# Empty expert slots left out of indirect transfers, and low weight parts split by rows, in a one-core Hyena, Fourier and mixture-of-experts block

## Chip, cores and metric

The kernel runs on one core of one Trainium2 chip. The metric is the device time of one execution in microseconds (us). About 0.3% can be told from no change.

## What is computed

One block for 2048 tokens of 1024 values: a mixer, then a mixture of experts, then a last norm. Cut to what matters here:

```
h    = rmsnorm(x)                        # 2048 x 1024
proj = h @ w_in                          # 3*512 Hyena columns, 512 Fourier columns
y1   = long convolution (FFT of 4096) of gated Hyena columns, 512 columns
y2   = real part of a 2-D FFT over tokens and 64 columns, 8 groups
x    = x + head_rmsnorm([y1, y2]) @ w_out
tok  = rmsnorm(x)
each token: best of 4 groups, best 2 of its 8 experts -> 4096 (token, weight) pairs, 32 experts
out[t] += weight * (silu(tok[t] @ w_gate[e]) * (tok[t] @ w_up[e])) @ w_down[e]
result = rmsnorm(x + out)
```

## The kernel before, in words

Products that must be exact to fp32 are made from a high and a low part (fp32r): hi x hi, hi x lo, lo x hi. The program is written in one order; a scheduler then puts each engine's instructions in a fixed order, earlier written work first where several are ready, and buffers with a tag are handed on when the last reader of the old content is through.

1. **Projection (0 to about 422 us).** `piece` (L323) multiplies cut weights with the transposed tokens `hhi`, `hlo`. The Hyena columns get a short convolution, go through DRAM and through the first step of the FFT (`ufirst`, L561).
2. **Residues and Fourier products (422 to 618 us).** `fourier(h, i)` (L674) makes 128 tokens x 256 columns of half `h` with 24 matmuls (L680): for each of 8 row blocks `d` of the weights hi x hi, then with the low weights, then with the low tokens. Half 0 has 16 products, the first six right at 422 us; half 1 has 16. Between them stand the 32 spectrum residues (`residue`, L756): nine matmuls each (L754; 15 for residue 0), two loads, casts and copies on ScalarE (ACT), six operations on VectorE (DVE, L782 once for each residue but the first) and one on GpSimd (POOL). In the program one residue follows each product, eight ahead of it at the start. The tables `su`, `sk`, `si` (L740) are loaded by POOL; their part 0 is read by residue 0 alone.
3. **Weights of a half.** `fweights(h)` (L664) takes the buffer "whl" for the high parts `wh` (two buffers) and "wl" for the low parts `wl` (one buffer), and for each column group `g` of 128: loads `wr` into "wraw" (one buffer) by SyncE's queue (SP, L670), cuts eight 128x128 pieces with ACT (`wh`, L309) and writes eight low pieces with DVE (`wl`, L310). `fweights(1)` stands in the program after product 4 of half 0.
4. **End of that stage.** With residue 31 done, buffers are opened for the Fourier mixer: `cs1` (a table, in the pool "fq"), `h5` (in "wraw"), `r0` (in the first row of `lg`). `mid`, two sums of `h5`, is made at L1093 and L1094 in the next pool.
5. **Mixer outputs and routing (618 to about 945 us).** `route` picks experts and ranks their tokens; `order` puts the experts in the order of their use, full ones first, the least filled of each group last. Then four lists over [128 slots x 32 experts] are written: `gia`, `gib` (rows to gather; an empty slot reads row 0) and `sia`, `sib` (rows to add to; an empty slot names one of 160 spare rows behind the 2048 rows of `X2`).
6. **Experts (945 to 1594 us, end at 1674 us).** For each expert: gather of 128 rows of 4 KB (`xg`, L987), for 18 of them also 32 overflow rows in quarters (`xo`, L990), transposes, `gate_up` (L1722), `down` (L1815), then a GpSimd DMA that adds the result into `X2` (L1821), and one for the overflow (L1758). Each waits for the one before. Weights stream in by SP. The last two experts (30, 31) run undivided: `ahead` (L1620) gathers their rows of `X2` once all additions have landed, `bulk` (L1581) reads all of `X2` again (L1588), norms and writes it; `finish` (L1626) adds the two experts' part, writes it to `X2` (L1635) and their output rows go out by a scatter (L1874) that has a bounds check already.

## Time and profile before

| | us |
|---|---|
| median of 3 runs | 1671.64 (1668.62 to 1673.2) |
| the profiled execution | 1675.47 |
| its span, first to last instruction | 1673.7 |
| mean granted TensorE clock, share of full | 0.982 |
| projection, to the first Fourier product | 0 to 422 |
| residues and Fourier products | 422 to 618 |
| mixer outputs and routing | 618 to 945 |
| experts and last norm | 945 to 1674 |

The stages' borders are read from the order of instructions in time. A row of a window gives, for a stretch of time, each engine's busy time in us, with the number of instructions that start in it in brackets; then the granted TensorE clock as a share of 2.4 GHz, the mean busy share of the 16 DMA engines, and GB/s. A row of instructions in time gives start, duration, engine, line, operation, output and input, a count, and in brackets the idle time before it and what ended that. Matmuls overlap, so the distance of their starts, not their duration, is what one costs.

### The profile page before, as it was taken

What the parts mean: (1) busy time and instruction counts of PE and PEld (TensorE: products, weight loads), DVE (VectorE), ACT (ScalarE), POOL (GpSimd) and SP (SyncE); (2) the same over time, 40 slices, a digit from 0 to 9 for tenths busy, and PEclk for the clock granted to TensorE, in tenths of its full rate; (3) what the DMA queues carried; (4) which work ended last, traced back from release to release, by engine and by line L of the source; (5) the groups of instructions that cost most, each with busy time, mean ns of one, the idle gap of its engine ahead of it and who ended that gap; (6) DMA issues with size and microseconds to landing.
All of it is one profiled execution on the core that took longest, in us unless ns stands there. A gap on an engine that the chain in (4) does not pass through costs nothing.

```text
span 1673.7 us, 27233 instructions
## 1 busy us (share of the span) xinstructions
PE 1574.7 (94%) x8995; PEld 1200.8 (72%) x8995; DVE 1192.6 (71%) x2162; ACT 1031.0 (62%) x1746; POOL 438.7 (26%) x515
## 2 busy tenths in 40 slices
PE   7999999999998999999999999999999999999992
PEld 5767776778887787876666567777777777777740
DVE  7667756533499966555877877888878888888825
ACT  8445667555698844414444467777777777777732
POOL 0202444332233220103434331222222222221112
PEclk9999999999998999999999999999999999999996
DMA  7245677699765587668778689999999999999997
GB/s 265 66 133 156 191 214 217 189 312 256 212 197 189 176 257 232 203 222 229 230 225 320 227 315 337 337 353 361 343 325 338 351 369 340 333 340 349 378 383 281
DMA packets 202447, 449.77 MB, mean 269 GB/s; under 512 B 27037, under 2 KB 83066, under 8 KB 201280
## 3 DMA queue, kind: packets, MB, share of 16 engines
q1 hardware_dynamic: 129176, 316.25, 53.5%
q0 software_dynamic: 39568, 106.07, 22.4%
q10 hardware_dynamic: 33560, 25.69, 4.7%
q8 instruction: 72, 1.18, 0.3%
q14 instruction: 71, 0.58, 0.1%
HBM read 346.05 MB, written 103.17 MB: 268 GB/s over the span
## 4 chain that ended last, share of the span: by engine, by line
PE 73%; DVE 11%; ACT 5%; DMA 4%; issue 3%; POOL 1%; ACTq 0%; DVEq 0%; POOLq 0%; SPq 0%
PE pa L1722 20%; PE py L1815 10%; PE psm L323 9%; PE psd L1055 8%; PE po L1738 4%; PE pm L680 3%; PE po L1754 2%; PE pstr L1685 2%; PE pa L1719 1%; DMA xt<-in_x 1%; POOL acc L513 1%; PE psEO L1075 1%; PE psm L680 1%; PE pstr L1779 1%; PE pseo L1138 1%
## 5 line engine op out<-in xcount | busy, mean ns | idle before, releaser
L1538 DVE TENSOR_TENSOR l<-w,h 128x1024 fp32r<-128x1024 f32 x352 | 425.7, 1223 | 80.0 <-ACT h L1537 60.4
L1537 ACT CAST h<-w 128x1024 fp32r<-128x1024 f32 x352 | 368.9, 1049 | 106.9 <-PE pa L1722 75.2
L323 PE MATMUL psm<-hhi,wt 128*128 128x512 f32 x768 | 249.9, 396 | 0.7 <-ACT hhi L425 0.5
L1722 PE MATMUL pa<-h,xh 128*128 128x512 f32 x464 | 185.6, 400 | 0.2 <-issue 0.2
L1722 PE MATMUL pa<-l,xh 128*128 128x512 f32 x464 | 181.9, 392 | 0.0
L1722 PE MATMUL pa<-h,xl 128*128 128x512 f32 x464 | 181.6, 391 | 0.0
L323 PEld LDWEIGHTS psm<-hhi,wt 128*128 128x128 f32 x768 | 144.7, 189 | 35.9 <-issue 4.0
L323 PE MATMUL psm<-hlo,wt 128*128 128x512 f32 x384 | 151.7, 395 | 0.4 <-DVE hlo L426 0.2
L987 POOL DMA_INDIRECT xg<-XR,gia x30 | 45.9, 1529 | 295.0 <-PE pstr L1685 154.9
L1722 PEld LDWEIGHTS pa<-h,xh 128*128 128x128 f32 x464 | 87.0, 188 | 30.9 <-issue 12.0
L1722 PEld LDWEIGHTS pa<-h,xl 128*128 128x128 f32 x464 | 87.1, 188 | 20.2 <-DVE xl L1690 0.4
L1722 PEld LDWEIGHTS pa<-l,xh 128*128 128x128 f32 x464 | 87.1, 188 | 18.4 <-issue 0.4
L1815 PE MATMUL py<-l,sh 128*128 128x512 f32 x240 | 98.6, 411 | 0.0
L1815 PE MATMUL py<-h,sh 128*128 128x512 f32 x240 | 97.6, 407 | 0.7 <-ACT sh L1783 0.7
L1815 PE MATMUL py<-h,sl 128*128 128x512 f32 x240 | 96.3, 401 | 0.0
L323 PEld LDWEIGHTS psm<-hlo,wt 128*128 128x128 f32 x384 | 72.8, 189 | 16.6 <-DVE hlo L426 1.0
L1758 POOL DMA_INDIRECT X<-yo,sib x18 | 37.2, 2064 | 166.0 <-DVE l L1538 110.9
L748 POOL TENSOR_TENSOR yl<-yl,yh 128x512 fp32r<-128x512 f32 x32 | 48.6, 1522 | 108.2 <-ACT yh L747 82.8
L1738 PE MATMUL po<-w,xot 128*32 128x256 f32 x1152 | 66.9, 381 | 0.0
L513 POOL TENSOR_TENSOR acc<-ab,acc 128x512 f32<-128x512 f32 x32 | 48.2, 1507 | 69.0 <-ACT ab L512 67.8
L347 ACT COPY u<-psm 128x512 f32<-128x512 f32 x48 | 28.1, 586 | 53.0 <-PE psm L323 52.7
L680 PE MATMUL pm<-wh,hhi 128*128 128x256 f32 x208 | 59.9, 289 | 0.8 <-ACT wh L309 0.8
(495 smaller groups left out, 3655.8 us busy)
## 6 DMA issues: line engine op xcount, KB each, us to landing
w<-in_w_gate SPq DMA_DIRECT2D x128, 512.0 KB
w<-in_w_up SPq DMA_DIRECT2D x128, 512.0 KB
w<-in_w_down SPq DMA_DIRECT2D x120, 512.0 KB
xt<-in_x SPq DMA_DIRECT2D x31, 512.0 KB
de<-in_c_decay SPq DMA_DIRECT2D x32, 256.0 KB
YK<-yk ACTq DMA_DIRECT2D x32, 256.0 KB
z<-zT POOLq DMA_DIRECT2D x32, 256.0 KB, 5.9
YZ<-yz SPq DMA_DIRECT2D x64, 128.0 KB
```

The lines of the kernel that those rows point to most:

```text
L323: T.matmul(pm, wt[:, a, d, :], b[q][:, d, :], start=n == 0, stop=n == 23)
L513: G.tensor_tensor(KS["acc"], ab, KS["acc"], op=ALU.add)
L680: T.matmul(pm, a[q][:, d, P * o:P * o + P], b[:, d, :], start=n == 0, stop=n == 23)
L748: e.tensor_tensor(yl, y, yh, op=ALU.subtract)
L987: G.indirect_dma_start(xg_[e], None, XR, bass.IndirectOffsetOnAxis(ap=ga[:, e:e + 1], axis=0))
L1055: T.matmul(pd, a[:, c, :], b[:, c, 512 * h:512 * h + 512], start=n == 0, stop=n == 11)
L1537: cuts.append(A.copy(h, raws[n]))
L1538: V.tensor_tensor(l, raws[n], h, op=ALU.subtract)
L1722: T.matmul(pa[m], x[:, 4 * k + c, :], y[:, f], start=d == 0 and q == 0, stop=d == 7 and q == 2)
L1738: T.matmul(po_[e][32 * j:32 * j + 32, 256 * m:256 * m + 256], xoT[e][:, b % 2, 2 * k + b // 2, :], w[:, 256 * j:256 * j + 256], start=b == ...
L1758: G.indirect_dma_start(X4, bass.IndirectOffsetOnAxis(ap=sib[:, d:d + 1], axis=0), yo, None, compute_op=ALU.add)
L1815: T.matmul(py[i], x[:, c, :], y[:, f], start=c == 0 and q == 0, stop=c == 3 and q == 2)
```

## The change

Two things are changed, and memory is laid out anew around the second.

- **Empty slots.** `gia` and `gib` are gone; gathers use `sia` and `sib`, whose empty slots point past the last token. All gathers, additions and writes of experts get a bounds check, so that rows out of bounds are left out. The gathers of the first two experts keep their own list (`gfix`) without such rows.
- **Low weights.** `wl` is split by rows: row blocks 0 to 3 in "wl" (now two buffers of half the size), row blocks 4 to 7 in "wm" (one buffer). `fweights` goes by row halves: load of both column groups, eight cuts, and for the first half the eight low pieces; the second half's low pieces are written by `rest`, called where the half's first product begins.
- **Layout.** Part 0 of the three tables goes to "wraw" (for `si` half of it), the rest to smaller tiles; nine loads in place of three. `cs1` goes to "wraw", `h5` and `r0` to "wl", `mid` to the first row of `lg`, made in two halves by `middle`: half 0 with residue 31 done, half 1 after product 14.

```diff
-        gia = cp.tile([P, NE], I32, name="gia")
-        gib = cp.tile([P, NE], I32, name="gib")
...
             def fweights(h):
                 wh = wp.tile([P, 8, 256], F32R, tag="whl", bufs=2, name="wh")
-                wl = wx.tile([P, 8, 256], F32R, tag="wl", bufs=1, name="wl")
-                for g in range(2):
-                    wr = wp.tile([P, 8, P], F32, tag="wraw", bufs=1, name="wr")
-                    S.dma_start(wr, Wp[2 * h + g])
-                    cutg(wh[:, :, P * g:P * g + P], wl[:, :, P * g:P * g + P], wr)
-                fw[h] = wh, wl
+                wls = [wx.tile([P, 4, 256], F32R, tag="wl", bufs=2, name="wl")]
+                def low(j):
+                    for d in range(4):
+                        for g in range(2):
+                            sl = slice(P * g, P * g + P)
+                            V.scalar_tensor_tensor(wls[j][:, d, sl], wr[:, g, d, :], g1[:, 4 * j + d:4 * j + d + 1],
+                                                   wh[:, 4 * j + d, sl], op0=ALU.mult, op1=ALU.subtract)
+                for j in range(2):
+                    wr = wp.tile([P, 2, 4, P], F32, tag="wraw", bufs=1, name="wr")
+                    for g in range(2):
+                        S.dma_start(wr[:, g], Wp[2 * h + g][:, 4 * j:4 * j + 4, :])
+                    for d in range(4):
+                        for g in range(2):
+                            A.activation(wh[:, 4 * j + d, P * g:P * g + P], wr[:, g, d, :], AF.Copy,
+                                         scale=g1[:, 4 * j + d:4 * j + d + 1])
+                    if j == 0:
+                        low(0)
+                def rest():
+                    wls.append(wx.tile([P, 4, 256], F32R, tag="wm", bufs=1, name="wm"))
+                    low(1)
+                    return wh, wls
+                fw[h] = rest
...
-            wh, wl = fw.pop(0)
+            wh, wl = fw.pop(0)()
...
-            for x, n in ((su, "c_su"), (sk, "c_sk"), (si, "c_si")):
-                G.dma_start(x, I[n].rearrange("x p h c -> p x h c"))
+            t0 = wp.tile([P, 1024], F32R, tag="wraw", bufs=1, name="t0")
+            su = [[t0[:, 192 * a:192 * a + 192] for a in range(2)]]
+            sk = [[t0[:, 384 + 256 * a:640 + 256 * a] for a in range(2)]]
+            si = [[t0[:, 896:1024], fp.tile([P, P], F32R, name="si0")]]
+            for x, n, w in ((su, "c_su", 192), (sk, "c_sk", 256), (si, "c_si", P)):
+                y = fp.tile([P, 2, w], F32R, name=n)
+                G.dma_start(y, I[n][1])
+                for a in range(2):
+                    G.dma_start(x[0][a], I[n][0, :, a])
+                x.append([y[:, a] for a in range(2)])
...
+            def middle(h):
+                x, y = (h5[k].rearrange("p (g c) -> p g c", g=2) for k in range(2))
+                g = slice(2 * h, 2 * h + 2)
+                V.tensor_tensor(v4(mid[:, 0:264])[:, g], x[:, :, 0:66], y[:, :, 0:66], op=ALU.add)
+                V.tensor_tensor(v4(mid[:, 264:512])[:, g], x[:, :, 66:128], y[:, :, 66:128], op=ALU.subtract)
...
                 if h:
-                    wh, wl = fw.pop(h)
+                    wh, wl = fw.pop(h)()
...
-                            css = {1: [fq.tile([P, 2, 2, 2, P], F32R, name="cs1")]}
+                            css = {1: [wp.tile([P, 2, 2, 2, P], F32R, tag="wraw", bufs=1, name="cs1")]}
...
-                            x = wp.tile([P, 2, 512], F32, tag="wraw", bufs=1, name="h5")
+                            x = wx.tile([P, 4, 256], F32, tag="wl", bufs=2, name="h5")
...
         def gather(e, part=(0, 1)):
-            ga, gb = (gfix[:, 0], gfix[:, 1]) if e < NFIX else (gia, gib)
+            ga, gb = (gfix[:, 0], gfix[:, 1]) if e < NFIX else (sia, sib)
...
-                G.indirect_dma_start(xg_[e], None, XR, bass.IndirectOffsetOnAxis(ap=ga[:, e:e + 1], axis=0))
+                G.indirect_dma_start(xg_[e], None, XR, at(ga[:, e:e + 1]), bounds_check=L - 1, oob_is_err=False)
...
-                        for u, x in enumerate((gia, gib)):
-                            first_rows(x, lt[:, u], u)
-                        V.tensor_copy(wsl, lt[:, 2:4])
...
+                        V.tensor_copy(wsl, lt[:, 2:4])
...
-                G.indirect_dma_start(za, None, X2, at(sia[:, e:e + 1]))
+                G.indirect_dma_start(za, None, X2, at(sia[:, e:e + 1]), bounds_check=L - 1, oob_is_err=False)
...
-                G.indirect_dma_start(X2, bass.IndirectOffsetOnAxis(ap=sia[:, e:e + 1], axis=0), yt, None, compute_op=ALU.add)
+                G.indirect_dma_start(X2, at(sia[:, e:e + 1]), yt, None, compute_op=ALU.add,
+                                     bounds_check=L - 1, oob_is_err=False)
```

The gather of `xo`, the addition of `yo` and the write of `za` change in the same way, the uses of the tables and of `wl` follow the new tiles, and L1093 and L1094 are gone.

## Rows read from the trace of the kernel before

**Rows 1.** The page's first part: busy us (share of the span) x instructions.

```profile
PE 1574.7 (94%) x8995; PEld 1200.8 (72%) x8995; DVE 1192.6 (71%) x2162; ACT 1031.0 (62%) x1746; POOL 438.7 (26%) x515
```

**Rows 2.** Windows, all engines: stretch, PE, PEld, DVE, ACT, POOL, clock, DMA, GB/s.

```profile
1008.00:1554.00 546.00, 546.00 (x3608) 416.75 (x3608) 450.96 (x476) 405.00 (x482) 125.57 (x78) 1.00 0.97 345
1586.00:1650.00 64.00, 52.58 (x142) 26.16 (x140) 28.87 (x57) 29.83 (x58) 14.44 (x18) 0.92 1.03 389
```

**Rows 3.** Instructions in time, PE: neighbouring matmuls of L754 and of L680.

```profile
443.64 0.39 PE L754 MATMUL U<-yh,su 128*128 128x512 f32 x1
443.87 0.40 PE L754 MATMUL U<-yl,su 128*128 128x512 f32 x1
...
600.06 0.28 PE L680 MATMUL pm<-wl,hhi 128*128 128x256 f32 x1
600.18 0.28 PE L680 MATMUL pm<-wh,hlo 128*128 128x256 f32 x1
```

**Rows 4.** Windows of L680 alone, then of L754 alone: PE, clock, DMA, GB/s.

```profile
500.00:520.00 20.00, 11.18 (x70) 1.00 0.65 208
520.00:545.00 25.00, 10.61 (x58) 0.80 0.60 188
...
590.00:618.00 28.00, 22.50 (x173) 1.00 0.77 239
...
500.00:520.00 20.00, 13.59 (x42) 1.00 0.65 208
520.00:545.00 25.00, 11.39 (x32) 0.80 0.60 188
...
590.00:618.00 28.00, 4.44 (x15) 1.00 0.77 239
```

**Rows 5.** Windows, all engines, before the change of halves and over it.

```profile
500.00:520.00 20.00, 19.46 (x112) 16.49 (x111) 19.41 (x28) 19.07 (x36) 9.08 (x5) 1.00 0.65 208
520.00:545.00 25.00, 19.08 (x90) 15.47 (x88) 20.74 (x39) 17.18 (x36) 7.47 (x5) 0.80 0.60 188
```

**Rows 6.** Low pieces (DVE), load (from the chain that ended last) and cuts (ACT).

```profile
521.40 3.20 DVE L310 SCALAR_TENSOR_TENSOR wl<-wr,vecs,wh 128x128 fp32r<-128x128 f32 x8
...
524.63 6.26 DMA wr<-Wp
...
530.91 2.44 ACT L309 ACTIVATE wh<-wr,vecs 128x128 fp32r<-128x128 f32 x8 [0.95 <-DMA wr<-Wp]
...
531.35 1.22 DVE L310 SCALAR_TENSOR_TENSOR wl<-wr,vecs,wh 128x128 fp32r<-128x128 f32 x4 [1.70 <-ACT wh L309]
...
533.32 1.14 DVE L310 SCALAR_TENSOR_TENSOR wl<-wr,vecs,wh 128x128 fp32r<-128x128 f32 x4
```

**Rows 7.** Instructions in time, DVE: L782, two successive residues, and the fifth after.

```profile
516.39 0.68 DVE L782 TENSOR_TENSOR ks<-U,ks 128x512 f32<-128x512 f32 x1
...
520.75 0.68 DVE L782 TENSOR_TENSOR ks<-U,ks 128x512 f32<-128x512 f32 x1
...
551.79 0.68 DVE L782 TENSOR_TENSOR ks<-U,ks 128x512 f32<-128x512 f32 x1
```

**Rows 8.** Instructions in time: first table load (POOL), first matmul of residue 0.

```profile
423.54 0.71 POOL L740 DMA_DIRECT2D su<-in_c_su  x1 [1.08 <-DVE cv L339]
...
442.24 0.39 PE L754 MATMUL K<-yh,sk 128*128 128x512 f32 x1
```

**Rows 9.** The end: POOL's additions, SP's reads in time; the checked scatter's group.

```profile
1589.14 2.39 POOL L1821 DMA_INDIRECT X<-yt,sia  x1 [6.53 <-ACT h L1537]
1600.77 1.55 POOL L1821 DMA_INDIRECT X<-yt,sia  x1 [9.24 <-DMA X<-yt,sia]
...
1610.07 16.57 SPq L1588 DMA_DIRECT2D xt<-X  x16
...
L1874 POOL DMA_INDIRECT out_y<-oa,sia x2: 981/1002/1023, 1659.3 to 1663.3; - x2
```

More of the change, by code (lines that the diff above doesn't have):

```diff
@@ L678, in fourier @@
                 for d in range(8):
-                    for a, b in ((hhi, wh), (hhi, wl), (hlo, wh)):
-                        T.matmul(pm, a[q][:, d, P * o:P * o + P], b[:, d, :], start=n == 0, stop=n == 23)
+                    for a, b in ((hhi, wh[:, d, :]), (hhi, wl[d // 4][:, d % 4, :]), (hlo, wh[:, d, :])):
+                        T.matmul(pm, a[q][:, d, P * o:P * o + P], b, start=n == 0, stop=n == 23)
                         n += 1
@@ L775, in residue @@
                     kp, up = kp[0], up[0]
-                    prod(kp, lambda a: sk[:, r, a, 64:192], kh, kl)
-                    prod(up, lambda a: su[:, r, a, 64:192], uh, ul)
+                    prod(kp, lambda a: sk[r][a][:, 64:192], kh, kl)
+                    prod(up, lambda a: su[r][a][:, 64:192], uh, ul)
                     lo, hi = slice(0, 64), slice(64, P)
@@ L885, in build @@
                         reverse(i - 13)
+                    if h and i == 14:
+                        middle(1)
                     while j0(i, h):
@@ L903, in build @@
                                 G.dma_start(css[1][0][:, c], I["c_ldft"][1][:, c, :, 0:2])
-                            x = wp.tile([P, 2, 512], F32, tag="wraw", bufs=1, name="h5")
+                            x = wx.tile([P, 4, 256], F32, tag="wl", bufs=2, name="h5")
                             for k in range(2):
-                                h5[k] = x[0:1, k]
-                                S.dma_start(h5[k][:, 0:256], RM[1 - k][3][0:1, 0:256])
+                                h5[k], r0[k] = x[0:1, k], x[0:1, 2 + k]
+                                S.dma_start(h5[k], RM[1 - k][3][0:1, 0:256])
                             lg = gp.tile([P, NT, 36], F32, name="lg")
                             lst = gp.tile([P, 2, 5, NE], F32, name="lst")
-                            x = lg.rearrange("p a b -> p (a b)")
-                            for k in range(2):
-                                r0[k] = x[0:1, 256 * k:256 * k + 256]
+                            mid = lg.rearrange("p a b -> p (a b)")[0:1, 0:512]
+                            middle(0)
                             jm = lst.rearrange("p a b c -> p (a b c)")[:, 0:P]
@@ L1090, in build @@
                 S.dma_start(altr, I["c_altr"])
-                mid = fo.tile([1, 512], F32, name="mid")
-                V.tensor_tensor(v4(mid[:, 0:264]), v4(h5[0])[:, :, 0:66], v4(h5[1])[:, :, 0:66], op=ALU.add)
-                V.tensor_tensor(v4(mid[:, 264:512]), v4(h5[0])[:, :, 66:128], v4(h5[1])[:, :, 66:128], op=ALU.subtract)
                 def pseo():
@@ L1615, in bulk @@
                 return [lambda g=g: end(g) for g in (4, 8, 12)]
-            def at(rows):
-                return bass.IndirectOffsetOnAxis(ap=rows, axis=0)
             def ahead(e):
                 za = fa.tile([P, D], F32, tag="q", bufs=2, name="za")
-                G.indirect_dma_start(za, None, X2, at(sia[:, e:e + 1]))
+                G.indirect_dma_start(za, None, X2, at(sia[:, e:e + 1]), bounds_check=L - 1, oob_is_err=False)
                 return za
@@ L1634, in finish @@
                     A.activation(oa[:, f], za[:, f], AF.Square, accum_out=ss[:, i:i + 1])
-                G.indirect_dma_start(X2, at(sia[:, e:e + 1]), za, None)
+                G.indirect_dma_start(X2, at(sia[:, e:e + 1]), za, None, bounds_check=L - 1, oob_is_err=False)
                 V.tensor_tensor(ss[:, 0:1], ss[:, 0:1], ss[:, 1:2], op=ALU.add)
```

20 lines of the change are left out of this document (10 added, 10 removed).

## The prediction, on record before the changed kernel ran

> **What bounds the kernel now.** I read the page first, then the windows, then the stage in which the diff moves work. The page [rows 1] says TensorE (PE) is busy 94% of the span, so time is gained only where PE stands still or runs at half clock. The windows of the whole core [rows 2] split the second half: from 1008 to 1554 us PE is busy for 546.00 of 546 us, and from 1586 to 1650 us the DMA share is 1.03 with PE at 52.6 of 64 us. So the gathers and additions of the expert loop lie behind PE until the last experts, and then the DMA engines and a chain of waits set the end.
>
> The stage from 442 to 618 us runs two kinds of work: 32 spectrum residues (L756, matmuls of L754, most of DVE and ACT) and the Fourier products (L680), which fill PE. Between neighbouring matmuls of one kind the starts lie 0.12 us apart for L680 and 0.23 us for L754 [rows 3]. Multiply by the counts of the windows [rows 4]: in 500 to 520 us PE did 70 x 0.12 + 42 x 0.23 = 18.1 us of work, 90%. In 520 to 545 us it did 58 x 0.12 + 32 x 0.23 = 14.3 us of 25, so 10.7 us are lost; at the 10% of the stretch before it would have been 2.5 us. **The hole costs PE about 8.2 us.** Part is standing still, part the clock: its mean is 0.80 there [rows 5], that is, for a while the lower level of 1.2 GHz in place of 2.4 GHz, after PE had run out of work.
>
> What made the hole: the low weights of column half 1 may be written only when the last product of half 0 has read the one buffer "wl". At 521.40 DVE writes the first eight pieces (3.20 us), only then is "wraw" free for the second load, which takes 6.26 us by the chain, then ACT cuts eight pieces (from 530.91 us, 2.44 us), then DVE writes the last eight [rows 6]. The residue cadence shows the same: L782 comes every 4.36 us (516.39 to 520.75), but its next five periods take 31.04 us [rows 7].
>
> **The change part by part.** *Weights of half 1.* The sixteen cuts and sixteen lows stay, but are ordered by rows: lows of rows 0 to 3 go to a second buffer "wl", with nothing of half 0 in their way; the load of rows 4 to 7 and its cuts follow. Only the eight lows of rows 4 to 7 ("wm", one buffer) still wait for the last product of half 0. So the load and the cuts leave the hole. What stays is eight DVE pieces, 3.20 us by the row. PE meanwhile has the first half of the next product, 12 matmuls x 0.12 = 1.4 us, and then waits at most 1.8 us; queued behind the lows on DVE are the residues' products, and PE's L754 waits for those. Term: 8.2 - 1.8 = 6.4 us. Bounds: below, 3.7 us, DVE's own account (31.04 - 5 x 4.36 = 9.24 us beyond the cadence, of which 3.20 + 1.22 + 1.14 = 5.56 us are lows that must be done anyway); above, the whole 8.2 us. I take 6.4, because the stage ends on PE: from 590 to 618 us it holds 173 products of L680 and only 15 of L754 [rows 4], so what counts is how much of L680 is left when the residues are through. That the moved work costs nothing elsewhere rests on DVE and ACT finding room between 450 and 520 us; they are busy 19.41 and 19.07 of 20 us there [rows 5], so this cover is thin, and a rival below takes it away.
>
> *SP and POOL.* Four loads of 512 KB become eight of 256 KB, some 0.3 us of SP's queue each, with slack. Those of half 1 now stand behind the release of t0, the tables of residue 0 in "wraw", so after that residue, near 450 us; the hole is at 520, hence nothing. The tables become nine loads on POOL instead of three, six of them behind the lows of half 0 that read "wraw". Before, the first was issued at 423.54 us and read at 442.24 [rows 8]: 18 us of room for six more issues of about 0.7 us each, so nothing again; cover gone, residue 0 slips one for one. cs1 goes to "wraw", its loads free to start before the residues end. The two sums "mid" become four smaller ones, earlier, on DVE after the residues; nothing either way.
>
> *Index lists.* Three DVE operations on 32 columns go, sia comes first; gather 2 reads it while PE is dense. The bounds check is already on the last scatter: 1.00 us on POOL, where an unchecked addition takes 1.55 [rows 9]. No cost.
>
> *Empty slots.* In the dense stretch, nothing. At the end: the additions of experts 28 and 29 are issued at 1589.14 and 1600.77 us, the second when the first has landed, and the reads of the result begin at 1610.07, when the second has [rows 9]: 20.9 us in line, ahead of the whole ending. Routed on the host, the reference fills 116 and 113 of the 128 slots of these two experts (103 and 91 of the last two), so 27 of 256 rows go. If the time between issue and landing, less 2.4 and 1.6 us of POOL, follows rows, that is 16.9 x 27/256 = 1.8 us; if what lands last is another row, nothing. The profile has no addition with fewer rows; I take 0.9, half way, and keep 0 and 1.8.
>
> The Trainium skill, "DMA: Bandwidth & Descriptors", section "The descriptor swizzle", deals the partitions of a 128-partition transfer in groups of four to the engines, so the empty slots from 113 up would all lie with four of sixteen engines, and the others would keep eight rows each. By that rule the last landing stays where it is, the term is 0 and the sum 6.4 us; no run here shows an engine's own rows.
>
> **Sum.** 6.4 + 0.9 = 7.3 us. The profiled execution took 1675.47 us (span 1673.7 and 1.8 around it) and stands 3.8 us above the median of 1671.64; it would come to 1668.2. Against the median: **1664.3 us**. About 0.3%, or 5 us, is what a measurement of this kernel can tell from no change.
>
> **Rivals.** *DVE sets the end of the stage* (chance 0.2). The second half of the lows is now written into the program after the residues of half 0, so DVE, full as it is, may take those residues first; the next product waits half done, PE idles beside the residues, and only DVE's 3.7 us are saved. For it: DVE at 97%. Against: 173 products after the residues. Time: 1671.6 - 3.7 - 0.9 = 1667.0.
>
> *Nothing arrives* (0.2). What PE gains at 545 us is lost behind it: from 590 to 618 us there are waits of other stages to meet, and no row shows how the rest takes an earlier start; or the order of instructions shifts and gives back as much. For it: PE loses 10% in 500 to 520 us as well, without such a cause. Time: 1671.6 less 0 to 2, so 1670.6.
>
> *Slower* (0.11). The place is ACT and DVE between 450 and 520 us. If cuts and lows of half 1 hold up the residues there one after the other, 2 x 2.44 + 3.20 = 8.1 us are added to the residue chain, the last eight lows still cost 3.2 at 520, and if the interleaving then falls out of step by one cadence, 4.4 more: 15.7 us against the 9.2 that the residues lost before, so 6.5 us more, less 0.9: 1677.2. It decides from 9.2 us of added delay on. For it: both engines at 95% and more. Against: the pieces come in ones, and L680 stays free to fill PE.
>
> *Forecast* (0.49): the hole closes but for a wait of up to 1.8 us.
>
> **How the numbers follow.** The forecast alone spans 1660 to 1666. Faster by over 0.3% is most of it, a third of the first rival (its 4.6 us lie at the bound), and little else: 0.58. Within: 0.31. Slower: 0.11. The range takes in the upper bound with both terms whole (8.2 + 1.8, and 3 us for a stage that runs on better than I know: 1658.5) and the rival without gain with a run above the median: 1673.0; the slower rival is what is left out, and some above the low end.
>
> **What would show it.** Right: in the profile after, lows of rows 0 to 3 near 460 us; no load of Wp after 500; eight lows alone at the change of halves, no PE wait over 2 us there, clock 1.00 throughout; 25 us there hold over 75 products of L680; the last L680 some 6 us earlier, and the start of the dense expert stretch as much. At the end, the distance from the addition of expert 28 to the first read of the result falls from 20.9 to about 20 us, or stays. Wrong: lows of rows 4 to 7 spread over later residues (first rival); the last L680 at 617 us with the hole gone (second); L782 periods of over 5 us between 450 and 520 (third); or tables landing after 442 us.

## The result and the profile after

The changed kernel takes 1683.18 us (median of 5 runs, 1680.28 to 1685.39) against 1671.64 us before (5 runs, 1668.62 to 1675.34): a ratio of 1.0062 with a 95% interval of 1.0041 to 1.0083. It is 11.5 us slower by the medians and 10.4 by the ratio, where 7 us faster was forecast. The profiled execution has a span of 1682.6 us, 8.9 more than before.

TensorE (PE) does the same work in the same busy time, by the first part of the page (it answers to [rows 1]):

```profile
PE 1574.5 (94%) x8995; PEld 1200.8 (71%) x8995; DVE 1196.6 (71%) x2161; ACT 1032.4 (61%) x1746; POOL 441.9 (26%) x521
```

So the 8.9 us are time in which PE stands still. To find them I count each stage from the first residue matmul (442.24 us before, 442.0 after; over all runs it moves between 438.7 and 444.6 us although nothing ahead of it differs much). The stage that the change edits ends for the rest of the program when the mixer can use its result; I take the first matmul of the row of alternating signs (`nyquist`, L1106 before, L1139 after), "Nyquist" below, 181.0 us after the first residue matmul before and 190.2 after: 9.2 us. From there to the order of the experts the kernel after is 0.9 us longer, the dense expert stretch 1.5 us shorter, the ending 0.5 us longer, and its start 0.2 us earlier: together the 8.9 us.

Residues and products both end late. The groups of the last residue products and of the Fourier products in the kernel before (L754, L680), then after (L779, L699); the two times are the first and the last start:

```profile
L754 PE MATMUL zp<-ph,si x64: 387/397/628, 448.5 to 599.8; 128*128 128x512 f32 x64
...
L680 PE MATMUL pm<-wh,hlo x208: 274/283/415, 448.1 to 617.3; 128*128 128x256 f32 x104
```

```profile
L779 PE MATMUL zp<-ph,c_si x62: 387/397/730, 454.6 to 609.8; 128*128 128x512 f32 x62
...
L699 PE MATMUL pm<-wh,hlo x208: 274/283/419, 447.1 to 626.4; 128*128 128x256 f32 x104
```

The windows of all engines say where (columns as in [rows 5]; the third row answers to its second):

```profile
465.00:485.00 20.00, 13.38 (x39) 7.31 (x38) 19.18 (x29) 18.93 (x38) 6.34 (x5) 0.91 0.55 167
500.00:520.00 20.00, 18.03 (x102) 14.77 (x101) 17.52 (x26) 18.03 (x38) 4.68 (x4) 1.00 0.62 197
520.00:545.00 25.00, 21.78 (x128) 18.10 (x127) 24.05 (x32) 21.24 (x40) 8.57 (x7) 1.00 0.58 184
546.00:588.00 42.00, 37.24 (x212) 32.22 (x211) 35.89 (x52) 30.96 (x58) 9.74 (x8) 0.92 0.61 187
```

The kernel before, in the first and the last of these stretches:

```profile
465.00:485.00 20.00, 19.28 (x108) 15.82 (x107) 19.07 (x27) 18.52 (x35) 7.10 (x5) 1.00 0.61 191
...
546.00:588.00 42.00, 38.74 (x227) 32.53 (x226) 39.95 (x55) 37.00 (x68) 12.12 (x10) 1.00 0.55 167
```

From 520 to 545 us the old hole is gone: 128 matmuls where there were 90, and the clock at 1.00. In its place stand two others. **The first hole** is at 465 to 485 us: 39 matmuls, where the kernel before has 108. PE's instructions in time show that not one Fourier product runs for 20.3 us, and that the clock falls to its lower level (a residue matmul of 0.40 us takes 0.63):

```profile
465.01 0.28 PE L699 MATMUL pm<-wh,hlo 128*128 128x256 f32 x1
...
480.22 0.63 PE L779 MATMUL zp<-pl,c_si 128*128 128x512 f32 x1
...
485.30 0.33 PE L699 MATMUL pm<-wh,hhi 128*128 128x256 f32 x1
```

PE waits for ScalarE (ACT). Products go into two buffers "pm", and a buffer is free when ACT has copied it out (L713). ACT's instructions in time: cuts of half 1 (L681) and then the first copy since 442 us, 20 us after the two buffers were full:

```profile
454.01 0.69 ACT L681 ACTIVATE wh<-wr,vecs 128x128 fp32r<-128x128 f32 x2
...
474.43 1.28 ACT L681 ACTIVATE wh<-wr,vecs 128x128 fp32r<-128x128 f32 x4
...
479.95 0.40 ACT L681 ACTIVATE wh<-wr,vecs 128x128 fp32r<-128x128 f32 x1
...
484.82 0.37 ACT L713 COPY rt<-pm 128x256 f32<-128x256 f32 x1
```

It is the fixed order of ACT's instructions that does this, not a wait. Of that order, condensed, only the cuts of half 1, the copies of products and the `zs` copy of each residue, before:

```
L309 ACTIVATE wh<-wr  (eight, the last ahead of the third of these)
L694 COPY rt<-psm     (the first six products)
L793 COPY zs<-zp      (residue 0)
L694 COPY rt<-pm      (first product in pm)
L793 COPY zs<-zp      (residues 1, 2, 3)
L694 COPY rt<-pm      (second)
L694 COPY rt<-pm      (third)
```

and after:

```
L713 COPY rt<-psm     (the first six products)
L818 COPY zs<-zp      (residue 0)
L681 ACTIVATE wh<-wr  x2
L818 COPY zs<-zp      (residues 1, 2, 3, 4)
L681 ACTIVATE wh<-wr  x5
L818 COPY zs<-zp      (residue 5)
L681 ACTIVATE wh<-wr
L818 COPY zs<-zp      (residue 6)
L713 COPY rt<-pm      (first product in pm)
L818 COPY zs<-zp      (residue 7)
L713 COPY rt<-pm      (second)
```

**The second hole** is at 546 to 588 us: PE 37.24 of 42 us at a mean clock of 0.92 (before 38.74 at 1.00). It is not a stretch without products, but one in which PE has gaps. There the lows of row blocks 4 to 7 come one by one between the pieces of residues, over 14 us, where before eight came in one block of 3.20 us [rows 6]. DVE's instructions of L672 in time:

```profile
543.51 0.70 DVE L672 SCALAR_TENSOR_TENSOR wm<-wr,vecs,wh 128x128 fp32r<-128x128 f32 x1
...
550.52 0.60 DVE L672 SCALAR_TENSOR_TENSOR wm<-wr,vecs,wh 128x128 fp32r<-128x128 f32 x2
...
554.64 1.28 DVE L672 SCALAR_TENSOR_TENSOR wm<-wr,vecs,wh 128x128 fp32r<-128x128 f32 x1
...
557.54 0.34 DVE L672 SCALAR_TENSOR_TENSOR wm<-wr,vecs,wh 128x128 fp32r<-128x128 f32 x1
```

The ending is as it was. POOL's additions and SP's reads in time, as in [rows 9]: 20.55 us from the addition of expert 28 to the first read, 20.93 before.

```profile
1597.91 2.00 POOL L1850 DMA_INDIRECT X<-yt,sia  x1 [6.92 <-ACT h L1568]
1609.45 1.55 POOL L1850 DMA_INDIRECT X<-yt,sia  x1 [9.54 <-DMA X<-yt,sia]
...
1618.46 16.61 SPq L1619 DMA_DIRECT2D xt<-X  x16
```

### The profile page after: what moved, and what is told of

The parts are those of the page before. It is cut to its first block, busy times and chain, and to the rows that moved or that the text cites. A ratio compares the mean times of both kernels' runs of the same rounds, so it can differ in the third digit from the quotient of the medians.

```text
span 1682.6 us, 27360 instructions
## 1 busy us (share of the span) xinstructions
PE 1574.5 (94%) x8995; PEld 1200.8 (71%) x8995; DVE 1196.6 (71%) x2161; ACT 1032.4 (61%) x1746; POOL 441.9 (26%) x521
## 4 chain that ended last, share of the span: by engine, by line
PE 70%; DVE 11%; DMA 6%; ACT 5%; issue 4%; POOL 2%; SPq 1%; ACTq 0%; POOLq 0%; DVEq 0%
PE pa L1750 19%; PE py L1844 10%; PE psm L321 8%; PE psd L1091 8%; PE po L1766 4%; PE pm L699 2%; PE po L1782 2%; PE pstr L1713 2%; POOL acc L511 2%; PE pa L1747 1%; DMA cs<-in_c_ldft 1%; PE psm L699 1%; PE pstr L1808 1%; PE psEO L1111 1%; PE pseo L1171 1%
## 5 line engine op out<-in xcount | busy, mean ns | idle before, releaser
L1023 POOL DMA_INDIRECT xg<-XR,sia x30 | 48.3, 1611 | 293.4 <-PE pstr L1713 168.4
L1750 PEld LDWEIGHTS pa<-h,xl 128*128 128x128 f32 x464 | 87.2, 188 | 20.2 <-issue 0.4
L321 PEld LDWEIGHTS psm<-hlo,wt 128*128 128x128 f32 x384 | 72.5, 189 | 16.6 <-DVE hlo L424 1.0
L773 POOL TENSOR_TENSOR yl<-yl,yh 128x512 fp32r<-128x512 f32 x32 | 45.0, 1409 | 119.5 <-ACT yh L772 109.1
L699 PE MATMUL pm<-wh,hhi 128*128 128x256 f32 x208 | 59.4, 286 | 0.0
```

The lines of the kernel that those rows point to most:

```text
L321: T.matmul(pm, wt[:, a, d, :], b[q][:, d, :], start=n == 0, stop=n == 23)
L699: T.matmul(pm, a[q][:, d, P * o:P * o + P], b, start=n == 0, stop=n == 23)
L773: e.tensor_tensor(yl, y, yh, op=ALU.subtract)
L1023: G.indirect_dma_start(xg_[e], None, XR, at(ga[:, e:e + 1]), bounds_check=L - 1, oob_is_err=False)
L1750: T.matmul(pa[m], x[:, 4 * k + c, :], y[:, f], start=d == 0 and q == 0, stop=d == 7 and q == 2)
```

## The experiments

The table gives each kernel's ratio to the kernel before, measured on the same chip, with its 95% interval; that ratio times 1671.64 us, to be held against the times in the expectations (the kernel before has medians of 1674.7 to 1676.3 us beside these runs); and three times from its trace in us after its own first residue matmul: the start of the last residue matmul, of the last Fourier product, and Nyquist. The three times are those of one profiled execution each and hold to 0.1 us as readings. *halfrows*, the last experiment, ran once and is not in the table.

| kernel | ratio (interval) | us | residue | product | Nyquist |
|---|---|---|---|---|---|
| before | 1 | 1671.6 | 157.6 | 175.1 | 181.0 |
| after | 1.0062 (1.0041 to 1.0083) | 1682.0 | 167.8 | 184.4 | 190.2 |
| slots | 0.9985 (0.9967 to 1.0004) | 1669.1 | 156.5 | 173.1 | 179.8 |
| weights | 1.0048 (1.0025 to 1.0072) | 1679.7 | 167.6 | 184.3 | 190.1 |
| t0wl | 1.0032 (1.0017 to 1.0047) | 1677.0 | 164.2 | 181.0 | 186.8 |
| early | 1.0020 (1.0002 to 1.0037) | 1675.0 | 163.1 | 179.9 | 185.7 |
| t0wl_early | 1.0016 (0.9998 to 1.0034) | 1674.3 | 156.7 | 170.5 | 181.4 |
| late8 | 1.0021 (1.0001 to 1.0040) | 1675.2 | 163.7 | 180.5 | 186.3 |
| fewer | 1.0023 (1.0009 to 1.0037) | 1675.5 | 154.5 | 160.7 | 183.4 |
| nolows | 0.9966 (0.9948 to 0.9983) | 1666.0 | 148.0 | 164.9 | 170.6 |
| slots_pool | 0.9993 (0.9975 to 1.0011) | 1670.5 | 157.1 | 174.5 | 182.3 |
| poolv | 1.0027 (1.0009 to 1.0046) | 1676.2 | 164.0 | 180.7 | 186.6 |
| zs0 | 1.0049 (1.0033 to 1.0065) | 1679.8 | 160.2 | 177.2 | 191.5 |
| zs0_early | 1.0023 (1.0005 to 1.0040) | 1675.5 | 154.3 | 169.8 | 183.8 |
| zs0_g | 1.0025 (1.0010 to 1.0041) | 1675.8 | 154.7 | 171.2 | 180.4 |

### Which part of the change

*slots* is the kernel before with the hunks on `gia`, `gib`, `at` and the bounds checks alone; *weights* has all the others.

> The kernel before with the empty slots' part alone (lists with bounds checks in gathers, reads and additions; gia and gib gone); the weights stay as before. Theory (the loss of 11 us lies in the Fourier stage): the stage from 442 to 618 us as before, last Fourier product at 617 us; the expert stretch at most some 1.5 us shorter (in the kernel after, the shift shrank from 9.9 us at its first gate matmul to 8.4 at its last), the tail as before (20.9 us from the addition of expert 28 to the first read): 1669.5 to 1671.6 us. Rival (the checks cost the loss): some 1680 us, with longer indirect issues on POOL in the expert stretch.

> The kernel before with the weights' part alone; gathers and additions stay as before. Theory: the whole loss, and the 1.5 us of the expert stretch on top: 1682 to 1685 us, last Fourier product near 626 us, no Fourier product on PE for about 20 us from 465 us on. Rival (the checks cost the loss): within 2 us of 1671.6.

The loss is the weights' part: its Nyquist is at 190.1 us, like the kernel after, and its time 8 us over before (2.3 us under the range expected). The empty slots bring about 2.5 us by the ratio, with an interval that just takes in nothing. In every trace that has them the expert stretch (first to last matmul of `gate_up`, L1722 before) is some 1.6 us shorter (629.4 to 629.6 against 631.1 to 631.2 us in the four kernels without); it is gained in the first 32 us after the experts are put in order, where the lists are written in another order and PE's instructions follow in another order too. What there gains it was not tried.

### Two causes, taken away one by one

*t0wl* puts the tables of residue 0 elsewhere, so that "wraw" is free for the first load of half 1 before the residues begin.

```diff
-wls = [wx.tile([P, 4, 256], F32R, tag="wl", bufs=2, name="wl")]
+wls = [wx.tile([P, 4, 256], F32R, tag="wl%d" % h, bufs=1, name="wl")]
...
-t0 = wp.tile([P, 1024], F32R, tag="wraw", bufs=1, name="t0")
+t0 = wx.tile([P, 1024], F32R, tag="wl1", bufs=1, name="t0")
...
-x = wx.tile([P, 4, 256], F32, tag="wl", bufs=2, name="h5")
+x = wx.tile([P, 4, 256], F32, tag="wl0", bufs=1, name="h5")
```

> The kernel after, but the tables of residue 0 lie in the second buffer wl (free until the lows of half 1) and not in wraw, so the first load of half 1 need not wait for residue 0. Theory (cuts of half 1 in the dense stretch take the place of the copies that free PE's two buffers pm): the first eight cuts of half 1 come before 442 us, the copies come every 5 us or so from 455 us on, PE has products throughout 465 to 485 us and its clock stays at 1.00 there; the hole of 6.9 us goes, the one at the change of halves stays: 1674 to 1678 us. Rival (the lows make DVE's chain of residues longer, the missing products only follow): all sixteen lows are still in the dense stretch, so 1680 us or more, the last residue near 609 us as in the kernel after.

*early* leaves the tables where they are and writes the lows of row blocks 4 to 7 with the cuts.

```diff
+wls.append(wx.tile([P, 4, 256], F32R, tag="wm", bufs=1, name="wm"))
+low(1)
+
 def rest():
-    wls.append(wx.tile([P, 4, 256], F32R, tag="wm", bufs=1, name="wm"))
-    low(1)
     return wh, wls
```

> The kernel after, but the lows of rows 4 to 7 of half 1 are written into the program with its cuts, ahead of the residues from 13 on; the tables of residue 0 stay in wraw. Theory (two holes, each with its own cause): the hole from 465 to 485 us stays (no Fourier product on PE for about 20 us), the one at the change of halves goes: the last Fourier product some 4 to 7 us earlier than in the kernel after counted from the first residue matmul (184.4 us there), the time 1676 to 1680 us. Rival (one cause, the late cuts; the second hole is only its echo): both holes stay, 182 us or more and 1682 us.

*t0wl_early* has both edits.

> As the run with the tables in wl, and the lows of rows 4 to 7 of half 1 are written into the program with the cuts, ahead of the residues from 13 on, and not at the start of half 1. Theory: the lows of rows 4 to 7 come as one block of some 3 us on DVE after the last product of half 0, the second hole goes too, and what was forecast arrives: last Fourier product at 611 to 613 us, 1663 to 1668 us. Rival (DVE's chain of residues sets the end): the last residue stays near 609 us and the time at 1675 us or more.

With the tables out of "wraw", PE has products throughout 465 to 485 us (106 matmuls, clock 1.00) and Nyquist comes 3.4 us earlier than in the kernel after. With the lows written early and the tables left, the first hole stays (20.7 us without a product) and the second goes: 4.5 us. With both, 8.8 us. So they are two causes, and with both gone 8.8 of the 9.2 us that the stage lost are back. By the ratios the three kernels are 5.0, 7.0 and 7.7 us ahead of the kernel after; these bear the order out but not the split, for each ratio has an interval of 2.5 to 3.5 us either way. The windows of all engines, t0wl, then early:

```profile
465.00:485.00 20.00, 18.47 (x106) 15.32 (x104) 19.21 (x30) 17.36 (x32) 4.46 (x4) 1.00 0.58 172
```

```profile
465.00:485.00 20.00, 14.39 (x40) 8.20 (x40) 18.91 (x28) 18.55 (x37) 5.43 (x4) 0.83 0.56 165
...
546.00:588.00 42.00, 38.21 (x233) 32.50 (x233) 39.26 (x59) 34.59 (x64) 11.04 (x10) 1.00 0.66 205
```

But what was forecast did not arrive in t0wl_early either. It has no stretch of PE of over 3.5 us without a product, its lows of row blocks 4 to 7 stand in one block of 3.23 us, its products end 4.6 us earlier than before, and its Nyquist lies where it was. My theory for this run (1663 to 1668 us) fell, and so did the rival (a last residue near 609 us). Behind its last product the chain of waits shows what PE waits for now:

```profile
605.40 0.43 PE rev L859 x2
605.83 0.64 PE rev L860 x2
606.47 0.37 POOL lst L1306
607.00 5.21 DMA rr<-RM,mir
...
615.84 0.70 DVE ab L893
...
616.58 0.81 PE pseo L1172 x2
```

The last mirrored read (`rr`) is issued at 607.00 us. The second of the eight starts at 595.80, when the last residue is through and its buffers are opened; it is so before as well (600.26 us). So there are two chains to the end of the stage, and before they end together: products, and residues with the reads behind them. The rows of the kernel before: the last read (L819) is issued at 610.88 us and lands 6.9 us later, at 617.8; the copy of the last product is through at 618.04, and the sum L838 waits for both.

```profile
610.88 0.95 POOL L819 DMA_INDIRECT rr<-RM,mir  x1 [1.50 <-DVE rr L840]
...
DMA to landing us min/median/max: 6.9/6.9/6.9
...
617.66 0.38 ACT rr L683
618.07 0.43 DVE rr L838
...
623.24 3.65 PE pseo L1106 x16
```

(By its trace t0wl_early should be level with before, by its runs it is 2.7 us behind, with an interval from 0.3 us ahead to 5.7 behind. One trace says how far the end can move by itself: the program of halfrows, the same as after's up to the additions, has its last residue and its last product where after has them, within 0.4 us, but Nyquist at 194.5 us in its one profile, with a mean clock of 0.83 from 620 to 640 us, and not at 190.2 with a clock of 1.00. So a difference of a few us in Nyquist alone, between two traces, proves little.)

### Is it the products or the residues

*fewer* leaves out the third factor in half 1's products, *nolows* the low weights of half 1 (its products use those of half 0).

```diff
-for a, b in ((hhi, wh), (hhi, wl), (hlo, wh)):
+for a, b in ((hhi, wh), (hhi, wl), (hlo, wh))[:2 if h else 3]:
```

> The kernel before, with the third factor (the high weight part times the low data part) left out of all sixteen products of half 1: 128 matmuls of 0.12 us, 15.4 us of PE's work, go from the Fourier stage. Theory (the residues on DVE and ACT, and the mirrored reads that start when the last residue is through, reach the end of the stage together with the products): the products end 8 to 13 us earlier, but the matmuls of the Nyquist row start at most 2 us earlier than 181.0 us after the first residue matmul; time 1669 to 1672 us. Rival (the products on PE set the end, as the prediction took it): the Nyquist row starts 8 us or more earlier and the time is 1659 to 1664 us.

```diff
-cutg(wh[:, :, P * g:P * g + P], wl[:, :, P * g:P * g + P], wr)
+if h:
+    for d in range(8):
+        A.activation(wh[:, d, P * g:P * g + P], wr[:, d, :], AF.Copy, scale=g1[:, d:d + 1])
+else:
+    cutg(wh[:, :, P * g:P * g + P], wl[:, :, P * g:P * g + P], wr)
```

> The kernel before, with the lower weight parts of half 1 left out (its products use those of half 0): sixteen DVE operations (5.6 us) and the wait for the buffer wl go, and the second load of weights no longer waits for the last product of half 0. Theory (residues and products share the end): this shortens both, the residues by the 9.2 us that they lost at the change of halves less what the cuts cost ACT, so the Nyquist row starts 5 to 9 us earlier after the first residue matmul than 181.0 us, time 1663 to 1667 us. Rival (nothing at the change of halves is on the path): within 2 us of 181.0 us, 1670 us or more.

*fewer* decides it for the products. Without 15.4 us of PE's work they end 14.4 us earlier, and the program is not faster but slower, by 0.23%: Nyquist is 2.4 us later. Both theories missed that sign. The chain that ended last shows PE waiting for the mirrored reads, and the window shows its clock at a mean of 0.73 after it ran dry. The last read is issued at 606.55 us and lands 9.5 us later (the stretch that the chain calls "issue" lies before that landing): 175.9 us after the first residue matmul, where before it is 175.6, though the last residue is 3.2 us earlier. So the reads end where they ended before, and what stands behind them takes longer.

```profile
606.55 5.58 DMA rr<-RM,mir
612.12 3.99 issue
616.12 0.43 DVE rr L838
...
620.00 0.81 PE pseo L1138 x2
...
623.55 5.56 PE pseo L1106 x16
```

```profile
590.00:620.00 30.00, 20.50 (x105) 17.64 (x104) 15.43 (x39) 9.43 (x18) 10.69 (x14) 0.73 0.85 263
```

Without the sixteen lows both chains are shorter, and the stage gains 10.4 us, 1.4 more than I gave it. In before, after, slots, weights, t0wl, early, late8, poolv and nolows Nyquist comes 22.5 to 23.3 us after the last residue; in the other six kernels of the table later than that, never sooner. In these nine the last product also comes 16.6 to 17.5 us after the last residue, so this regularity alone does not tell the two chains apart, and no run shortens the residues and their reads alone.

### Do the cuts crowd out the copies

*late8* writes the weights of half 1 four turns of the loop later.

```diff
-if h == 0 and i == 4:
+if h == 0 and i == 8:
     fweights(1)
```

> The kernel after, but the weights of half 1 are written into the program behind product 8 of half 0 and not behind the fourth turn of its loop, so that the copies of three more products stand ahead of them. Theory (the cuts, ahead of the copies in the program, take the gaps of a full ACT, and two buffers pm then leave PE without a product): the hole does not go, it moves behind the eighth product in pm (a run of 32 residue matmuls in a row there, 38 before), and the stage stays 7 us or more longer than before: Nyquist row 187 to 192 us after the first residue matmul, 1680 to 1685 us. Rival (only the place next to residue 0 and its tables is bad): PE has products throughout, Nyquist row at 184 us or less.

The hole moves: no product runs from 506.72 to 523.66 us (16.9 us; the window shows 30 matmuls and a clock of 0.79), and there is none at 465. Nyquist (186.3 us) is just under the theory's range and the time (1675.2 us) well under it, so the hole costs less here; it is still 2 us more than the rival allowed.

```profile
507.00:523.00 16.00, 12.20 (x30) 6.30 (x31) 14.17 (x20) 14.91 (x29) 3.98 (x3) 0.79 0.53 153
```

### Can the lows leave VectorE

*slots_pool* is slots with the lows of half 1 on POOL, *poolv* is t0wl_early with the same and with the copies of half 0's products on DVE.

```diff
-V.scalar_tensor_tensor(wl, wr, g, wh, op0=ALU.mult, op1=ALU.subtract)
+G.tensor_scalar(wr, wr, g, None, op0=ALU.mult)
+G.tensor_tensor(wl, wr, wh, op=ALU.subtract)
```

> The kernel before with the empty slots' part, and the sixteen lows of half 1 on POOL (two operations each); buffers and loads as before, so the hole at the change of halves stays. Theory (the residues set the end): DVE gives up 5.6 us, the residues pass the hole, the last one at 150 to 153 us after the first residue matmul, the Nyquist row at 173 to 177 us, 1664 to 1668 us, if the products do not end later than before (175.1 us). Rival (POOL's lows take longer than DVE's and the next product waits for them): products end at 178 us or later and the time is 1674 us or more.

> The kernel after with both cures (tables of residue 0 in wl, lows of rows 4 to 7 early), and more: the sixteen lows of half 1 go from DVE to POOL (two operations each) and the copies of half 0's products from ACT to DVE. Theory (the stage ends 22.5 us after the last residue, and the residues go at the pace of DVE and ACT together): DVE gives up some 8 us and takes some 4, ACT gives up 4, so the last residue lies 3 to 5 us earlier than in the run with both cures (156.7 us after the first residue matmul), the Nyquist row at 175 to 179 us, 1664 to 1670 us. Rival (POOL, which also makes a lower part for each residue, becomes the pace, or slows DVE beside it): last residue at 157 us or later, 1674 us or more.

Neither gained. In slots_pool the residues still end at 157.1 us, and neither theory nor rival had the time: what DVE gives up it loses waiting at the hole (busy for 21.89 us from 530 to 560 us, 25.49 in slots). In poolv they end 7.2 us later than in t0wl_early, as the rival had it. The groups of DVE and POOL instructions from 442 to 605 us (busy, mean ns, idle before), t0wl_early's sum first, say where that comes from. The sum L815, which reads two operands from SBUF, takes 988 ns where L811 of t0wl_early took 730 (L785 before 756); the two other DVE operations of that kind got no slower (850 and 721 ns, 913 and 762 in t0wl_early), so together they cost some 5 us more over 32 residues. L814, one of whose operands is in PSUM, is unchanged at 684. The twelve copies cost DVE 5.0 us, the sixteen lows that it gave up were 6.5 in t0wl_early, and its wait for ACT's copies ahead of each residue grew from 3.3 to 8.0 us. A low on POOL costs 946 + 633 ns against DVE's 409 before.

```profile
L811 DVE TENSOR_TENSOR ks<-ks 128x512 f32<-128x512 f32 x32 | 23.4, 730 | 0.3
```

```profile
L815 DVE TENSOR_TENSOR ks<-ks 128x512 f32<-128x512 f32 x32 | 31.6, 988 | 0.5
...
L814 DVE TENSOR_TENSOR ks<-U,ks 64x512 f32<-64x512 f32 x31 | 21.2, 684 | 1.0
```

```profile
L676 POOL TENSOR_SCALAR wr<-wr,vecs 128x128 f32<-128x128 f32 x8 | 7.5, 946 | 0.6 <-ACT wh L685 0.6
L677 POOL TENSOR_TENSOR wl<-wr,wh 128x128 fp32r<-128x128 f32 x8 | 4.8, 637 | 2.9 <-PE zp L784 2.9
```

### The forecast, made true

*zs0* puts the tables of residue 0 into the two buffers "zs", so that both cuts and the first lows of half 1 fit ahead of the residues; *zs0_early* adds the edit of early; *zs0_g* further sends four large loads of the next stage (two of L1048, two of L1215 in zs0_early) through POOL's queue.

```diff
-t0 = wp.tile([P, 1024], F32R, tag="wraw", bufs=1, name="t0")
-su = [[t0[:, 192 * a:192 * a + 192] for a in range(2)]]
-sk = [[t0[:, 384 + 256 * a:640 + 256 * a] for a in range(2)]]
-si = [[t0[:, 896:1024], fp.tile([P, P], F32R, name="si0")]]
+ta, tb = (fp.tile([P, 512], F32R, tag="zs", bufs=2, name="t0") for a in range(2))
+su = [[tb[:, 192 * a:192 * a + 192] for a in range(2)]]
+sk = [[ta[:, 256 * a:256 * a + 256] for a in range(2)]]
+si = [[tb[:, 384:512], fp.tile([P, P], F32R, name="si0")]]
```

> The kernel after, but the tables of residue 0 lie in the two buffers zs (free until the first zp is copied), so that all sixteen cuts and the lows of rows 0 to 3 of half 1 stand ahead of the residues; the lows of rows 4 to 7 are written early as in the run early. Theory (the loss is the cuts and lows of half 1 among the residues, which set the end of the stage; the forecast needs them out of there): no stretch of PE without a product over 5 us, the lows of rows 4 to 7 in one block of 3.2 us, the last residue 5 to 8 us earlier than before (150 to 153 us after the first residue matmul), the Nyquist row at 173 to 176 us, and with the 1.5 us of the expert stretch 1662 to 1667 us. Rival (closing the hole gives nothing, the residues' pace is the same without it): last residue at 156 us or later, the Nyquist row at 179 us or later, 1669 us or more.

> As zs0_early, but the lows of rows 4 to 7 are written at the start of half 1, as in the kernel after. Theory (late lows by themselves open the second hole): 32 residue matmuls in a row at the change of halves, the lows there in ones over 10 us or more, the Nyquist row 4 to 9 us later than in zs0_early, 1668 to 1675 us. Rival (with the cuts out of the way the place of eight lows no longer matters): within 2 us of zs0_early.

> As zs0_early, but the first two loads of the mixer's output weights and the first two of the tokens for the sum (four of 512 KB or a little less) go through POOL's queue, behind the mirrored reads, and not through SP, where they started at 606.87 to 609 us, ahead of the last three mirrored reads. Theory (in zs0_early these loads share the DMA engines with the last mirrored reads, and that is what gives the gain back at the end): from the last residue to the Nyquist row 22 to 25 us again (29.5 in zs0_early, 23.4 before), the Nyquist row at 176 to 180 us, 1666 to 1672 us. Rival (the mirrored reads wait for something else, such as the stores of the late products): 28 us or more, within 2 us of zs0_early.

In zs0_early the change of halves is what the prediction drew: one block of lows, no stretch of over 2.7 us without a product there, and from the first to the last L782 (L808 there) 139.9 us instead of 146.8. Of these 6.9 us 2.3 are lost at the start (the first of them comes 7.8 us after the first residue matmul, 5.5 before, and PE is without a product for 8.5 us there, 5.8 before, more than the theory allowed); the last residue is 3.3 us earlier, between the ranges of theory and rival, and the last product 5.3. And then the end takes it back: 29.5 us from the last residue to Nyquist, and a time in the rival's range. In the chain there the sixth mirrored read takes 8.38 us to land; in zs0_g, with the four loads behind the reads, the last one takes 2.77, and Nyquist is at 180.4 us. Over the reads whose landing is seen the median is 7.2 us in zs0_early and 4.4 in zs0_g. Both lose time on POOL as well: the issue of the fifth read takes 4.52 us, the others 0.95 to 1.06, and the last three stand behind it, so that the last leaves 15.5 and 16.4 us after the last residue matmul, 11.1 before. What lengthens that issue was not tried. The low block in zs0_early, the fifth read's issue, then the reads in the chains of zs0_early and of zs0_g:

```profile
524.24 3.23 DVE L672 SCALAR_TENSOR_TENSOR wm<-wr,vecs,wh 128x128 fp32r<-128x128 f32 x8
...
605.01 4.52 POOL L845 DMA_INDIRECT rr<-RM,mir  x1 [3.69 <-DVE rr L874]
...
609.85 8.38 DMA rr<-RM,mir
```

```profile
611.75 2.77 DMA rr<-RM,mir
```

So the theory on the loads was right that the reads land sooner without them, and still missed: from the last residue to Nyquist it is 25.7 us, 22 to 25 expected, and zs0_g is no faster, for from Nyquist to the order of the experts it is 4.1 us longer than zs0_early, now that those loads come late. zs0 shows the late lows by themselves: no product from 530.29 to 546.63 us, and Nyquist 7.7 us behind zs0_early, as the theory had it, with a time 5 us past its range.

### The empty rows at the end

*halfrows* is the kernel after with the main additions bounded at token 1024, which leaves out 107 of the 229 filled rows of experts 28 and 29.

```diff
-G.indirect_dma_start(X2, at(sia[:, e:e + 1]), yt, None, compute_op=ALU.add,
-                     bounds_check=L - 1, oob_is_err=False)
+G.indirect_dma_start(X2, at(sia[:, e:e + 1]), yt, None, compute_op=ALU.add,
+                     bounds_check=L // 2 - 1, oob_is_err=False)
```

> The kernel after, with the bound of the main additions at token 1024 and not 2048, so about half of the rows of each addition are left out (in every engine's share, if the Trainium skill, page DMA: Bandwidth & Descriptors, section The descriptor swizzle, holds here). Theory (the landing of an addition does not follow its rows near the end): from the addition of expert 28 to the first read of the result 19 to 20.6 us, as in the kernel after (20.6). Rival (it follows the rows): 12 to 14 us, and the time 7 to 8 us shorter.

From the addition of expert 28 to the first read it takes 17.72 us, 2.8 less than after (one profile):

```profile
1603.01 1.55 POOL L1850 DMA_INDIRECT X<-yt,sia  x1 [7.12 <-ACT yt L1849]
1612.37 1.55 POOL L1850 DMA_INDIRECT X<-yt,sia  x1 [7.82 <-DMA X<-yt,sia]
...
1620.73 9.51 SPq L1619 DMA_DIRECT2D xt<-X  x11
```

Neither range held: 9.36 us from the one addition to the next (11.54 after, 11.0 to 11.5 in all kernels that leave the empty slots out), 8.36 from there to the read (9.01 after, 9.0 to 9.3). In all, the kernels that leave the empty slots out have 20.2 to 20.7 us, those that keep them 20.0 to 20.9, so 27 rows fewer show nothing, and 107 fewer save 2.8.

The Trainium skill, "DMA: Bandwidth & Descriptors", section "The descriptor swizzle", deals partitions in groups of four to sixteen engines, eight each; it gives this for a transfer into 128 partitions, and here the rows leave them. By that rule, with the routing of the reference and the kernel's order of slots, the fullest engine keeps 8 of 8 rows when the empty slots are left out, and in halfrows 7 for expert 28 and 6 for expert 29. A landing that follows the fullest engine would then stay where it is with the empty slots left out, as it did; but in halfrows the first addition, whose fullest engine keeps 7, lands some 2 us sooner, and the second, whose fullest keeps 6, not quite 1. The rule by itself does not give these two times, and what sets a landing stays open. "In every engine's share" in the expectation was too coarse: by the rule the engines keep between 1 and 7 rows.

## Why the prediction was wrong

- **"I take 6.4, because the stage ends on PE."** In the order of the prediction this step failed first, and it is why nothing is gained where the loss is cured. The 173 matmuls of products from 590 us on were read as a queue on PE that a shorter hole would shorten. They were the cover of a chain that ended with them: last residue, seven mirrored reads (the last landing at 617.8 us, the last product copied out at 618.0), sums, cast. fewer takes 14.4 us off the products and Nyquist does not come earlier; t0wl_early and zs0_early take 4.6 and 5.3 off, and it does not either. The trace had it: seven of the eight mirrored reads behind the last residue (from 600.26 us on) and the last L680 (617.3 us) were both there, and no step asked what else ended near 618; the rival "Nothing arrives" (0.2) spoke of "waits of other stages to meet" there, and named none. What closing the hole is worth by itself no run shows: in zs0_early the last residue is 3.3 us earlier, near the lower bound of 3.7, and none of it is left at Nyquist.
- **"That the moved work costs nothing elsewhere"**, with the cover called thin, failed next, and it made the kernel slower: the 9.2 us of the stage. Of the loads the prediction said that the tables' release puts them "near 450 us; the hole is at 520, hence nothing". The first did leave SP at 448.93 us, but what hangs on a load is not done with it: its cuts ran from 454 to 480 us, its lows one by one from 463 to 499, the second load left at 499.71, and its cuts ran from 503 to 507. What the cuts displaced was not thought of at all: the copies that free PE's two buffers, written behind them in the program. By t0wl, early and both together the two holes cost 3.4, 4.5 and 8.8 us.
- **The rival "Slower"** had the place (ACT and DVE between 450 and 520 us) and the chance 0.11. It priced a delay of residues and a lost step, 6.5 us, and said against itself that "L680 stays free to fill PE". L680 was what stopped.
- **"DVE sets the end of the stage"** said that the second lows might be taken behind residues of half 0. That happened (543 to 558 us). The rival priced it as a gain forgone, and it was a loss of 4.5 us.
- **The tail's 0.9** was nothing, its lower bound. The 1.6 us that the empty slots did bring lay in the dense stretch, where the prediction had "nothing".
- **What held:** the hole at 520 to 545 us went (clock 1.00, 82 matmuls of L699 where over 75 were asked). The tables' nine loads, SP's queue and POOL's issues cost nothing that shows; where the tables lie did (t0wl). Of the signs of being wrong named beforehand, two appeared: "lows of rows 4 to 7 spread over later residues" and "L782 periods of over 5 us between 450 and 520".

No version that does all of the work beats the kernel before beyond its interval (nolows, which leaves the low weights of half 1 out, does); slots comes nearest, at 0.9985 (0.9967 to 1.0004).

## What to carry to other kernels

Before a stall is priced, list every chain that reaches the end of the stage and the slack between them; leaving out part of one chain's work in a trial kernel measures this in one run. Work that is moved out of a hole into a stretch where two engines are busy 95% displaces something, and under a scheduler that prefers earlier written work it displaces what is written last, so look up who waits for that. A buffer pair between a busy engine and the one that drains it needs the drain's place in the order kept.

## What the hardware showed that was not expected

- Less work made the program slower, by 0.23% (0.09 to 0.37): in fewer PE ran dry, its mean granted clock was 0.73 from 590 to 620 us, and the matmuls behind took longer. The Nyquist group (16 matmuls) took 5.56 us in the chain there and 3.65 before.
- A DVE operation on two SBUF operands is slower where it meets POOL's work. In poolv 16 of the 32 sums L815 overlap in time with one of POOL's tensor operations and take 1290 ns in the mean, the other 16 take 684; L814, with one operand in PSUM, takes 684 in both cases. The Trainium skill, "SBUF — State Buffer", section "SBUF: two separate sides", says that such a DVE operation and a POOL operation hold a shared pair of ports one after the other; the rows agree.
- One DVE low piece takes 334 to 1281 ns in the kernel after, placed singly. In the blocks of eight (3.20 to 3.23 us) of before, t0wl_early and zs0_early seven take 339 to 352 ns and the fifth 1352 to 1384; why is not shown.
